# Input projection and gates as block products in a stage of their own, with outputs passed through HBM

## The chip, the cores and the metric

The kernel runs on one core of one Trainium2 chip. The metric is the device time of one execution in microseconds, the median of several runs. PE is TensorE's matmul unit, DVE VectorE, ACT ScalarE, POOL GpSimd and SP the engine that issues most transfers. HBM is the memory off the core, PSUM the memory that PE accumulates into.

## The reference

One layer of a decoder trunk for 512 prompt tokens (one sequence) and 64 sample tokens (8 sequences of 8), with the same weights, in fp32:

```python
xn = rmsnorm(h, lw['g_mix'])
z = xn @ lw['w_in']                                    # 1024 -> 512 + 1024 + 512
u_pool, u_rnn, q = ...
gates = jax.nn.sigmoid((xn @ lw['w_gate'] + lw['b_gate']))   # 1024 -> 3 x 1024
y_pool, new_pool = pool_mixer(u_pool, ...)
y_rnn, ... = rglru(u_rnn, ...)
y_attn = cross_attn(q, m_k, m_v)                       # m_k, m_v from 256 memory tokens
merged = (gates[:, :, 0] * (y_pool @ lw['w_br_pool'])
          + gates[:, :, 1] * (y_rnn @ lw['w_br_rnn'])
          + gates[:, :, 2] * (y_attn @ lw['w_br_attn']))
h = h + merged @ lw['w_out']
xn2 = rmsnorm(h, lw['g_ffn'])
gv = xn2 @ lw['w_up']
...
h = h + (jax.nn.gelu(g_conv) * val) @ lw['w_down']
```

The outputs are the two groups' normalised h, the memory keys and values, and the state rows that the convolutions, the pooling and the recurrence carry on.

## The kernel before

The 576 tokens lie along the free axis and features along the 128 partitions, so that x is 8 tiles of 128 x 576. All large matmuls take fp32 in two parts: `hi` is the value rounded to the type that PE takes in one pass (ACT copies it, L111), `lo` the value less `hi` (DVE, L112), and each product of 128 input features is three matmuls, wh·xh, wh·xl and wl·xh (`mm3`, L197). A column tile of 576 tokens is worked in two halves of 288 (or 256 and 320), so that one output tile of 128 features from all 1024 inputs is 8 x 3 x 2 = 48 matmuls.

The program has two stages. The mix stage holds the projections, the three branches, the gates and the merge, the second stage (`op_ffn`) the output projection, the second norm, the conv-FFN and the final norm. The order of the mix stage is written out in the string `MIX` (L1221), one letter for an operation and digits for its tile: `a` loads x and scales it by g_mix, `x` computes the reciprocal root mean square of each token (rstd), `r` and `p` are the projections of RG-LRU and pooling tiles, `g` a gate tile, `c R A B` the steps of the RG-LRU (convolution, its two gates, decay, scan), `w d o` those of pooling, `m K M k V` the memory keys and values, `Q S T P s t v z` attention, `b` a product of a branch with its weights, gated and merged. `h H` bring in x again and split the merged tiles. The builder's scheduler may move instructions of neighbouring operations past each other; each engine then runs its own list in order.

The projections multiply x scaled by g_mix but not by rstd, which comes in as each result leaves PSUM: `op_gate` multiplies by it on DVE (L492) and then takes the sigmoid on ACT (L493), `scaled_evac` does it for RG-LRU and pooling (L285, L288). So PE can begin on projections before any norm is known. Class `Weights` loads each weight tile of 512 KB on SP's queue (two raw buffers) and splits it on ACT and DVE (three buffers each for hi and lo). There are 16 tiles of `w_in` and 24 of `w_gate`. They and all tiles between stay in the core's own memory.

## Time and profile before

| what | value |
|---|---|
| median of 3 runs | 948.49 us (948.09 to 950.51) |
| the profiled execution, its own time | 947.94 us |
| span of the profiled execution | 946.0 us |
| PE busy in the span | 919.5 us (97%) |
| mean granted TensorE clock | 0.996 of 2.4 GHz |
| mix stage | 0 to 450.7 us |
| output projection to the end (`op_ffn`) | 450.7 to 946.0 us |

The span runs from the first to the last instruction of the core; the execution's time is 1.9 us longer. The listed length of a matmul overlaps that of its neighbours, so that what one costs is read where many stand in a row in the chain. PE is busy nearly throughout; the other engines have idle time in every stretch.

### The profile page before, as it was taken

The page shows a single profiled execution, that of the slowest core. Times are in us where ns is not written, and L with a number is a line of the kernel's source. Part 1 is how long each engine was busy: PE and PEld are TensorE (multiplying, and loading weights), DVE is VectorE, ACT ScalarE, POOL GpSimd, SP SyncE. Part 2 cuts the span into 40 slices and gives each one's busy share as a digit, 9 for nine tenths or more (in the row PEclk, how much of TensorE's full clock was granted, in tenths as well). Part 3 has the DMA queues.
Part 4 walks back from the last instruction along what each step waited for, and adds up shares of the span by engine and source line. Part 5 has one row for each costly group of instructions (what it writes and reads, how often), then busy time and mean ns, then how long its engine had stood idle before and what let it go on. Part 6 is the DMA issues. An engine that isn't in the chain of part 4 may idle for free.

```text
span 946.0 us, 17081 instructions
## 1 busy us (share of the span) xinstructions
PE 919.5 (97%) x6924; PEld 903.0 (95%) x6924; DVE 621.9 (66%) x974; ACT 472.2 (50%) x745; POOL 200.9 (21%) x302
## 2 busy tenths in 40 slices
PE   6999999999999999999999999999999999999995
PEld 6999999999999979899999999999999999999995
DVE  7979864656434656237466998676676676676644
ACT  6455948496222546325455465444444444444443
POOL 5224221127113110022222232111111111111131
PEclk9999999999999999999999999999999999999998
DMA  7422222344233353533637255454454454453202
GB/s 234 140 79 68 75 71 69 94 146 133 81 112 98 124 202 127 187 122 112 211 83 158 90 163 155 124 145 134 125 143 135 128 141 137 123 142 110 84 30 100
DMA packets 39662, 116.73 MB, mean 123 GB/s; under 512 B 4608, under 2 KB 8704, under 8 KB 39584
## 3 DMA queue, kind: packets, MB, share of 16 engines
q1 hardware_dynamic: 34496, 100.19, 31.3%
q0 software_dynamic: 4000, 14.28, 8.6%
q8 instruction: 54, 0.88, 0.4%
q10 hardware_dynamic: 1088, 1.18, 0.4%
q14 instruction: 24, 0.20, 0.1%
HBM read 111.58 MB, written 4.05 MB: 122 GB/s over the span
## 4 chain that ended last, share of the span: by engine, by line
PE 86%; DVE 6%; issue 2%; DMA 2%; ACT 2%; POOL 1%; SPq 0%; DVEq 0%; ACTq 0%; POOLq 0%
PE pb_ffn L901 25%; PE ps_gate L197 15%; PE pd_ffn L987 13%; PE ps_branch L197 10%; PE pb_ffn L806 5%; PE ps_rnn_mm L197 3%; PE ps_q L197 3%; PE pb_ffn L1134 3%; PE ps_pool_mm L197 2%; PE pq_rnn_gate L197 1%; PE pq_k_mm L197 1%; PE ps_v L557 1%; DMA cv_spv<-in_cv 1%; DMA wr_start<-in_w_gate 1%; DVE wl_ffn L112 1%
## 5 line engine op out<-in xcount | busy, mean ns | idle before, releaser
L901 PE MATMUL pb_ffn<-b_ffn,wh_ffn 128*128 128x288 f32 x768 | 155.3, 295 | 0.0
L901 PEld LDWEIGHTS pb_ffn<-b_ffn,wh_ffn 128*128 128x128 f32 x768 | 123.3, 188 | 0.1
L901 PE MATMUL pb_ffn<-b_ffn,sh_ffn 128*128 128x288 f32 x576 | 119.3, 299 | 2.4 <-DVE b_ffn L112 1.3
L901 PE MATMUL pb_ffn<-b_ffn,wl_ffn 128*128 128x288 f32 x384 | 112.9, 294 | 0.0
L901 PEld LDWEIGHTS pb_ffn<-b_ffn,sh_ffn 128*128 128x128 f32 x576 | 92.0, 188 | 4.4 <-DVE b_ffn L112 1.7
L901 PE MATMUL pb_ffn<-b_ffn,sl_ffn 128*128 128x288 f32 x288 | 84.7, 295 | 0.2 <-DVE sl_ffn L112 0.2
L901 PEld LDWEIGHTS pb_ffn<-b_ffn,wl_ffn 128*128 128x128 f32 x384 | 72.2, 188 | 0.0
L111 ACT ACTIVATE wh_ffn<-wr_ffn 128x1024 fp32r<-128x1024 f32 x44 | 46.7, 1061 | 39.0 <-PE pb_ffn L901 37.7
L111 ACT ACTIVATE sh_ffn<-R_ffn 128x512 fp32r<-128x512 f32 x72 | 45.0, 626 | 26.1 <-PE pb_ffn L901 19.4
L987 PE MATMUL pd_ffn<-xb_ffn,wh_ffn 128*128 128x288 f32 x320 | 55.7, 295 | 1.0 <-ACT xb_ffn L111 1.0
L987 PE MATMUL pd_ffn<-xa_ffn,wh_ffn 128*128 128x288 f32 x320 | 55.6, 295 | 0.0
L901 PEld LDWEIGHTS pb_ffn<-b_ffn,sl_ffn 128*128 128x128 f32 x288 | 54.1, 188 | 0.4 <-DVE sl_ffn L112 0.4
L112 DVE TENSOR_TENSOR wl_ffn<-wr_ffn,wh_ffn 128x1024 fp32r<-128x1024 f32 x44 | 54.1, 1230 | 0.2
L111 ACT ACTIVATE wh_branch<-wr_branch 128x1024 fp32r<-128x1024 f32 (+1 forms) x24 | 22.0, 917 | 62.7 <-PE ps_gate L197 27.4
L974 POOL TENSOR_TENSOR v_ffn<-v_ffn,ext_ffn 128x576 f32<-128x576 f32 x24 | 36.0, 1499 | 79.7 <-ACT ext_ffn L963 77.1
L112 DVE TENSOR_TENSOR sl_ffn<-R_ffn,sh_ffn 128x512 fp32r<-128x512 f32 x72 | 51.1, 711 | 0.6 <-ACT sh_ffn L111 0.6
L112 DVE TENSOR_TENSOR wl_ffn<-R_ffn,wh_ffn 128x1024 fp32r<-128x1024 f32 x22 | 26.9, 1224 | 36.4 <-ACT wh_ffn L111 36.4
L856 POOL DMA_DIRECT2D wr_ffn<-in_w_up x21 | 18.7, 892 | 142.5 <-DMA wr_ffn<-in_w_up 102.0
L111 ACT ACTIVATE wh_ffn<-R_ffn 128x1024 fp32r<-128x1024 f32 x22 | 23.3, 1060 | 50.8 <-PE pb_ffn L901 47.0
L987 PEld LDWEIGHTS pd_ffn<-xb_ffn,wh_ffn 128*128 128x128 f32 x320 | 46.8, 188 | 1.2 <-ACT xb_ffn L111 1.2
L987 PEld LDWEIGHTS pd_ffn<-xa_ffn,wh_ffn 128*128 128x128 f32 x320 | 46.9, 188 | 0.0
L959 DVE SCALAR_TENSOR_TENSOR gc_ffn<-ext_ffn,par,gc_ffn 128x592 f32<-128x592 f32 x48 | 41.4, 862 | 6.1 <-ACT gc_ffn L957 6.1
(510 smaller groups left out, 2434.8 us busy)
## 6 DMA issues: line engine op xcount, KB each, us to landing
R_ffn<-in_w_up SPq DMA_DIRECT2D x24, 512.0 KB, 3.8
wr_ffn<-in_w_down SPq DMA_DIRECT2D x24, 512.0 KB, 4.2
wr_ffn<-in_w_up SPq DMA_DIRECT2D x23, 512.0 KB, 3.7
wr_ffn<-in_w_up POOLq DMA_DIRECT2D x21, 512.0 KB, 6.3
R_ffn<-in_w_up SPq DMA_DIRECT2D x24, 256.0 KB, 4.0
wr_gate<-in_w_gate SPq DMA_DIRECT2D x10, 512.0 KB, 3.3
ck_sscore<-in_ck SPq DMA_DIRECT2D x8, 512.0 KB, 4.5
cv_spv<-in_cv SPq DMA_DIRECT2D x8, 512.0 KB, 5.0
```

Source lines behind the costliest of these rows:

```text
L111: nc.scalar.activation(hi, src, AF.Copy)
L112: nc.vector.tensor_tensor(lo, src, f(hi), ALU.subtract)
L197: nc.tensor.matmul(out[:, c, : hs.stop - hs.start], a[:, ks], b[:, hs], start=(first and k == 0 and i == 0), stop=(last and k == K - 1 and ...
L557: nc.tensor.matmul(vps[:, mt, :], a[:, ms], b[:, ws], start=(k == 0 and i == 0), stop=(k == 7 and i == 2))
L806: nc.tensor.matmul(p_[:, :TH], a[:, ks], x[:, b], start=(k == 0 and i == 0), stop=(k == 7 and i == 2))
L856: nc.gpsimd.dma_start(SR[j], w2(wu[j][:, 1:3]), accum_op=ALU.add)
L901: nc.tensor.matmul(p_[:, :TH], a[:, ks], b[:, k, :], start=(first and k == 0 and i == 0), stop=(k == 3 and i == 2), skip_group_check=not f ...
L959: nc.vector.scalar_tensor_tensor(gc[:, :592], ext[:, q_ : q_ + 592], pc(cw + q_), gc[:, :592], ALU.mult, ALU.add)
L974: nc.gpsimd.tensor_tensor(v, v, ext[:, :T], ALU.mult)
L987: nc.tensor.matmul(p_[:, c, :TH], a[:, ks], b[:, hs], start=(k == 0 and i == 0), stop=(k == NFB - 1 and i == 2),)
L1134: nc.tensor.matmul(p_[:, :n], a[:, ks], b[:, cs], start=(k == 0 and i == 0), stop=(k == NFB - 1 and i == 2),)
```

## The change

The 40 column tiles of `w_in` and `w_gate` become 20 pairs. Both stand as blocks: the weights of a pair as 2 x 2 (two halves of the inputs by two tiles), x as 2 x 2 (two halves of the inputs by two halves of 288 tokens). Each pair is computed by seven products of blocks (512 inputs x 128 outputs by 288 tokens) where the plain way has eight, from sums and differences of blocks: forms of x are made once (`N11 N21 N22 T1 T2 T3 T4`, negated or summed blocks, each split into hi and lo), those of the weights for each pair, and the seven results are added and subtracted, in PSUM where signs allow, otherwise as they leave it. A product is 4 x 3 = 12 matmuls of 288 columns.

- All of this stands in a new operation `op_xstage`, first in `MIX`. It begins with the memory keys and values (which came later before), loads x in two halves of tokens, and normalises each half before any product.
- Table `XP` gives the order of the 20 pairs (`g` gate, `r` RG-LRU, `p` pooling, `q` attention queries), table `XTRA` what is done beside which pair: the RG-LRU's and pooling's steps in pairs 4 to 18.
- For each pair, SP loads 512 KB and 256 KB of weights (`load_X`) and 512 KB for the sums (`load_S`), to which POOL's queue adds another 512 KB by an accumulating transfer. From pair 4 on, the low part of the upper weight blocks is no DVE subtraction: ACT writes hi, then -hi into lo, and a second accumulating transfer adds the weights (`prep_A`).
- Gates, queries, the RG-LRU's and pooling's results and the keys and values are stored to scratch in HBM (28 tiles of 128 x 576, 8 of 128 x 600, 4 of 128 x 576, and the keys and values). The 24 branch products and attention follow in a stage that loads them back; `op_gate` there is a load and a sigmoid.
- `op_ffn` keeps its work.

```diff
+NPX = 3
+XP = (
+    ("g", 0, 0), ("g", 0, 1), ("g", 0, 2), ("g", 0, 3), ("r", 0), ("p", 0), ("g", 1, 0), ("r", 1), ("g", 1, 1), ("p", 1),
+    ("r", 2), ("g", 1, 2), ("g", 1, 3), ("r", 3), ("q", 0), ("q", 1), ("g", 2, 0), ("g", 2, 1), ("g", 2, 2), ("g", 2, 3),
+)
+XTRA = {
+    (4, 0): "L", (5, 0): "c0", (5, 1): "c1", (6, 1): "R0 R1 A0 A1", (7, 0): "B0 B1", (7, 1): "w0 d0", (8, 0): "c2 o0",
+    (8, 1): "c3 w1 d1", (9, 1): "R2 R3 A2 A3 o1", (10, 0): "B2 B3", (10, 1): "w2 d2", (11, 0): "c4 o2", (11, 1): "c5",
+    (12, 0): "w3 d3", (12, 1): "R4 R5 A4 A5 o3", (13, 0): "B4 B5", (14, 0): "c6", (14, 1): "c7",
+    (15, 1): "R6 R7 A6 A7", (16, 0): "B6 B7", (17, 1): "y0 y1", (18, 1): "y2 y3",
+}
...
+        def load_X(j):
+            AR[j] = raw()
+            nc.sync.dma_start(AR[j], w2(wx[j][:, 2:4]))
+            A2[j] = fs.tile([P, 512], F32, tag="a22", name=nm("a22"), bufs=2)
+            nc.sync.dma_start(A2[j], wx[j][:, 0])
+
+        def load_S(j, tag="xa"):
+            SR[j] = xu(tag, [1152], F32)[:, :1024]
+            nc.sync.dma_start(SR[j], w2(wx[j][:, 0:2]))
+            nc.gpsimd.dma_start(SR[j], w2(wx[j][:, 1:3]), accum_op=ALU.add)
+
+        def prep_A(j):
+            WA[j] = hi, lo = ring()
+            if j <= NPX:
+                split_to(hi, lo, AR[j])
+            else:
+                nc.scalar.activation(hi, AR[j], AF.Copy)
+                nc.scalar.activation(lo, f(hi), AF.Copy, scale=-1.0)
+                nc.gpsimd.dma_start(lo, w2(wx[j][:, 2:4]), accum_op=ALU.add)
+
+        def prep_S2(j):
+            r = AR[j]
+            nc.vector.tensor_tensor(r[:, :512], r[:, :512], SR[j][:, :512], ALU.add)
+            W1[j, 6] = single()
+            split_to(*W1[j, 6], r[:, :512])
+
+        def prep_S(j):
+            WS[j] = ring()
+            split_to(*WS[j], SR[j])
+
+        def prep_22(j):
+            W1[j, 4] = single()
+            split_to(*W1[j, 4], A2[j])
+
+        def prep_S4(j):
+            r = AR[j]
+            nc.vector.tensor_tensor(r[:, 512:], r[:, 512:], r[:, :512], ALU.add)
+            W1[j, 3] = single()
+            split_to(*W1[j, 3], r[:, 512:])
+
+        def prod(p_, w, c0, x, first=True):
+            wh, wl = w
+            xh, xl = B[x]
+            for k in range(4):
+                ks = slice(c0 + k * P, c0 + (k + 1) * P)
+                for i, (a, b) in enumerate(((wh, xh), (wh, xl), (wl, xh))):
+                    nc.tensor.matmul(
+                        p_[:, :TH], a[:, ks], b[:, k, :],
+                        start=(first and k == 0 and i == 0), stop=(k == 3 and i == 2),
+                        skip_group_check=not first,
+                    )
...
+        def done(j):
+            kind, a = XP[j][0], XP[j][1:]
+            if kind in OFF:
+                return
+            for i in range(2):
+                n = 2 * a[-1] + i
+                name = f"q{n}" if kind == "q" else f"g{a[0]}{n}"
+                nc.sync.dma_start(spill(name, [P, T]), S.pop(("out", j, i)))
...
+        def P1(j):
+            C["b6", j] = bank()
+            prod(C["b6", j], WA[j], 0, "N11")
+            C["p1", j] = act_copy(C["b6", j])
...
+        def P4(j):
+            p_ = C.pop(("b6", j))
+            prod(p_, W1.pop((j, 4)), 0, "T4", first=False)
+            for o, sl in halves(j, 1, 0):
+                if j < NPX:
+                    nc.vector.tensor_tensor(o, sl(p_), sl(C["u2", j]), ALU.add)
+                else:
+                    nc.scalar.activation(o, sl(p_), AF.Copy)
+            del C["u2", j]
+            done(j)
...
+            else:
+                P1(j)
+                if more:
+                    prep_A(n)
+                P5(j)
+                if more:
+                    prep_S2(n)
+                P6(j)
+                P2(j)
+                if more:
+                    prep_S(n)
+                P7(j)
+                extras((j, 0))
+                P3(j)
+                if more:
+                    prep_22(n)
+                P4(j)
+                if more:
+                    prep_S4(n)
+                ld(n + 2, n + 3)
+            extras((j, 1))
...
     def op_gate(b, m):
-        p_ = wmm(("w_gate", 8 * b + m), S["xg"], H288)
-        g = (tg if b < 2 else te if m < 4 else ty)(T)
-        nc.vector.tensor_tensor(v2(g), p_[:, :, :TH], v2(S["rb"]), ALU.mult)
+        g = MD["gl"].tile([P, T], F32, tag="gl", name=nm("gl"))
+        nc.sync.dma_start(g, SP[f"g{b}{m}"])
         nc.scalar.activation(g, g, AF.Sigmoid, bias=pc(C_BG + 8 * b + m))
```

DVE's list at the start before: splits of the first weights (`wl_start`) and of x as it arrives (`xa_start`, `xb_start`); the norm (`e_rstd_x`) comes behind them.

```order
L112 TENSOR_TENSOR wl_start<-wr_start,wh_start 128x256 [waits DMAHW1_49,Activation_49]
L282 SCALAR_TENSOR_TENSOR xa_start<-e_start,par,xa_start 128x576 [waits DMAHW2_49,DMAHW0_49,Activation_49]
L112 TENSOR_TENSOR wl_start<-wr_start,wh_start 128x256 [waits DMAHW3_49,Activation_49]
L282 SCALAR_TENSOR_TENSOR xb_start<-e_start,par,xb_start 128x576 [waits DMAHW4_49,Activation_49]
L112 TENSOR_TENSOR wl_start<-wr_start,wh_start 128x256 [waits DMAHW5_49,Activation_49]
L282 SCALAR_TENSOR_TENSOR xa_start<-e_start,par,xa_start 128x576 [waits DMAHW6_49,Activation_49]
L112 TENSOR_TENSOR wl_start<-wr_start,wh_start 128x256 [waits DMAHW7_49,Activation_49]
L282 SCALAR_TENSOR_TENSOR xb_start<-e_start,par,xb_start 128x576 [waits DMAHW0_49,Activation_49]
L282 SCALAR_TENSOR_TENSOR xa_start<-e_start,par,xa_start 128x576 [waits DMAHW1_49,Activation_49]
```

DVE's list now, shortly before the first product of the main loop (`xb_`, `xa_xstage` with 1152 elements are blocks of x, `pd` the broadcast rstd, `sl` low parts of pair weights, `b_90` the low part of T2, `b_104` that of T3):

```order
L486 TENSOR_TENSOR xb_xstage<-xb_xstage,pd_xstage 128x1152 [waits PE_49]
L486 TENSOR_TENSOR xb_xstage<-xb_xstage,pd_xstage 128x1152 [waits DMAHW6_49]
L783 TENSOR_TENSOR xa_xstage<-xb_xstage,xa_xstage 128x1152 [waits DVE_49]
L116 TENSOR_TENSOR sl_xstage<-wr_xstage,sh_xstage 128x512 [waits Activation_49]
L784 TENSOR_TENSOR xb_xstage<-xb_xstage,xa_xstage 128x1152 [waits DVE_49]
L116 TENSOR_TENSOR sl_xstage<-wr_xstage,sh_xstage 128x512 [waits Activation_49]
L793 TENSOR_TENSOR xb_xstage<-xb_xstage 128x1152
L116 TENSOR_TENSOR b_90_xstage<-xb_xstage,b_89_xstage 128x1152 [waits Activation_49]
L116 TENSOR_TENSOR b_104_xstage<-xb_xstage,b_103_xstage 128x1152 [waits Activation_49]
```

These rows stand behind 53 others of the same list, the splits of the memory tokens and of the eight key and value weights, the squares of x and the first two forms. On PE, the first products of the pairs follow the memory matmuls, and product P6 of pair 0 (`b_89` and `b_90` are T2) takes what the list above ends with:

```order
L548 MATMUL pb_xstage<-b_60_xstage,wh_xstage 128x288 [waits PE_49,Activation_49]
L548 MATMUL pb_xstage<-b_61_xstage,wh_xstage 128x288
L548 MATMUL pb_xstage<-b_89_xstage,sh_xstage 128x288 [waits PE_49]
L548 MATMUL pb_xstage<-b_90_xstage,sh_xstage 128x288 [waits DVE_49]
L548 MATMUL pb_xstage<-b_89_xstage,sl_xstage 128x288
L548 MATMUL pb_xstage<-b_89_xstage,sh_xstage 128x288
L548 MATMUL pb_xstage<-b_60_xstage,wl_xstage 128x288 [waits DVE_49]
```

The second matmul of P6 waits for DVE's row of `b_90`.

ACT's list before around the two gates of RG-LRU tile 2 (`e_rnn_gate` from PSUM `pq_rnn_gate`; `hab` weights; `wh` high parts of weights; `e_rnn_a` the decay; ACT_TABLE_LOAD stands where the function's table changes):

```order
L409 ACT_TABLE_LOAD [waits PE_49]
L409 ACTIVATE e_rnn_gate_1035<-pq_rnn_gate_1036,par 128x300 [waits Pool_49]
L493 ACTIVATE g_gate_2_1032<-g_gate_2_1032,par 128x576 [waits DVE_49]
L409 ACTIVATE e_rnn_gate_1035<-pq_rnn_gate_1041,par 128x300 [waits PE_49]
L409 ACTIVATE e_rnn_gate_1046<-pq_rnn_gate_1047,par 128x300 [waits PE_49]
L111 ACTIVATE e_pool_d_1076<-pd_pool_d_1070 128x576
L409 ACTIVATE e_rnn_gate_1046<-pq_rnn_gate_1052,par 128x300 [waits PE_49]
L111 ACTIVATE hab_rnn_conv_1656<-rab_rnn_conv_1654 128x256 [waits DMAHW4_49]
L111 ACTIVATE wh_gate_3_1173<-wr_gate_3_1171 128x1024 [waits DMAHW7_49,PE_49,Activation_49]
L111 ACTIVATE e_rnn_conv_1152<-e_rnn_conv_1147 128x600 [waits DVE_49,Pool_49]
L111 ACTIVATE e_pool_d_1162<-pd_pool_d_1156 128x576
L418 ACT_TABLE_LOAD
```

ACT's list now, from the last evacuation of pair 6 (L677) on; `u_xstage` is the evacuation of a pair's product:

```order
L677 ACTIVATE xa_xstage<-pb_xstage 128x288 [waits PE_49]
L342 ACT_TABLE_LOAD
L342 ACTIVATE e_xstage<-pd_xstage,par 128x300 [waits PE_49] x2
L605 ACTIVATE u_xstage<-pb_xstage 128x288 [waits PE_49]
L342 ACTIVATE e_xstage<-pd_xstage,par 128x300 [waits PE_49] x2
L115 ACTIVATE hab_xstage<-rab_xstage 128x256 [waits DMAHW4_49]
L342 ACTIVATE e_xstage<-pd_xstage,par 128x300 [waits DMAHW3_49,PE_49]
L342 ACTIVATE e_xstage<-pd_xstage,par 128x300 [waits PE_49]
L342 ACTIVATE e_xstage<-pd_xstage,par 128x300 [waits DMAHW4_49,PE_49]
L351 ACT_TABLE_LOAD [waits Activation_49]
L351 ACTIVATE e_xstage<-e_xstage,nsp_88 128x600 [waits Pool_49]
L342 ACT_TABLE_LOAD
```

The gates of two tiles now follow each other with few other rows between them, and the evacuations of the next pair's products (L605) stand in the same list. Up to the last evacuation of pair 7 there are 31 instructions in this interval: 4 evacuations of 288 columns, 8 sigmoids of 300, 5 table loads, 2 exponentials, 2 tangents, 2 squares and 2 square roots of 600, and copies of 1024, 576, three of 512 and one of 256.

PE in a steady pair before, one gate:

```order
L197 MATMUL ps_gate_0_522<-xa_start,wh_pool_mm_376 128x288 x4
L197 MATMUL ps_gate_0_522<-xa_start,wl_pool_mm_377 128x288 x2
L197 MATMUL ps_gate_0_522<-xb_start,wh_pool_mm_376 128x288 x4
L197 MATMUL ps_gate_0_522<-xb_start,wl_pool_mm_377 128x288 x2
L197 MATMUL ps_gate_0_522<-xa_start,wh_pool_mm_376 128x288 x2
```

and now, from the end of one pair to the start of the next (`b_115`, `b_116` T4; `b_60`, `b_61` N11; `wl` the low part that the accumulating transfer fills):

```order
L548 MATMUL pb_xstage<-b_116_xstage,sh_xstage 128x288
L548 MATMUL pb_xstage<-b_115_xstage,sl_xstage 128x288
L548 MATMUL pb_xstage<-b_60_xstage,wh_xstage 128x288
L548 MATMUL pb_xstage<-b_61_xstage,wh_xstage 128x288
L548 MATMUL pb_xstage<-b_60_xstage,wl_xstage 128x288 [waits DMASW7_49]
L548 MATMUL pb_xstage<-b_60_xstage,wh_xstage 128x288
L548 MATMUL pb_xstage<-b_61_xstage,wh_xstage 128x288
```

The third matmul of a pair's first product waits for a transfer on a POOL queue (DMASW); the weights' low part before came from DVE.

## Rows read from the trace of the kernel before

**Rows 1.** The page: span, and busy time of each engine

```profile
span 946.0 us, 17081 instructions
...
PE 919.5 (97%) x6924; PEld 903.0 (95%) x6924; DVE 621.9 (66%) x974; ACT 472.2 (50%) x745; POOL 200.9 (21%) x302
```

**Rows 2.** Stretches: PE, PEld, DVE, ACT, POOL busy (x); clock; DMA share; GB/s

```profile
0.00:24.00 24.00, 15.72 (x85) 14.31 (x85) 17.21 (x25) 16.27 (x26) 12.05 (x36) 1.00 0.70 231
...
100.00:150.00 50.00, 50.00 (x373) 49.67 (x373) 35.47 (x46) 35.09 (x52) 11.08 (x20) 1.00 0.23 70
...
400.00:451.00 51.00, 49.76 (x372) 49.32 (x371) 28.63 (x42) 20.59 (x35) 11.40 (x6) 1.00 0.39 127
```

**Rows 3.** The chain that ended last, 0 to 60 us: start, us, what

```profile
5.45 6.63 DMA wr_start<-in_w_gate
...
34.79 6.40 PE ps_rnn_mm L197 x48
```

**Rows 4.** The same chain from 300 to 455 us

```profile
302.93 5.67 PE pq_k_mm L197 x48
...
323.26 11.14 PE ps_v L557 x48
...
450.69 4.39 PE pb_ffn L806 x31
```

**Rows 5.** The longest wait of PE up to 451 us: total, times, longest

```profile
PE ps_rnn_mm L197 <- ACT xa_start L281: 5.9, 1, 5.9
```

**Rows 6.** ACT by shape: busy us, mean ns of one | idle before it

```profile
L111 ACT ACTIVATE sh_ffn<-R_ffn 128x512 fp32r<-128x512 f32 x72 | 45.0, 626 | 26.1 <-PE pb_ffn L901 19.4 <-DVE R_ffn L873 6.3
...
L111 ACT ACTIVATE wh_gate<-wr_gate 128x1024 fp32r<-128x1024 f32 x16 | 16.9, 1057 | 19.3 <-PE ps_branch L197 8.4 <-PE ps_rnn_mm L197 5.3 <-issue 4.3
L409 ACT ACTIVATE e_rnn_gate<-pq_rnn_gate,par 128x300 f32<-128x300 f32 x32 | 15.2, 507 | 3.4 <-PE pq_rnn_gate L197 3.1
...
L913 ACT ACTIVATE u_ffn<-pb_ffn 128x288 f32<-128x288 f32 x24 | 9.8, 410 | 16.0 <-PE pb_ffn L901 16.0
...
L409 ACT ACT_TABLE_LOAD x5 | 6.4, 1283 | 0.1
L418 ACT ACTIVATE e_rnn_a<-e_rnn_gate,nsp 128x600 f32<-128x600 f32 x8 | 6.4, 797 | 0.1
...
L420 ACT ACTIVATE e_rnn_gate<-e_rnn_a 128x600 f32<-128x600 f32 x8 | 5.6, 701 | 0.2
```

**Rows 7.** DVE by shape, columns as in the group before

```profile
L112 DVE TENSOR_TENSOR wl_ffn<-wr_ffn,wh_ffn 128x1024 fp32r<-128x1024 f32 x44 | 54.1, 1230 | 0.2
L112 DVE TENSOR_TENSOR sl_ffn<-R_ffn,sh_ffn 128x512 fp32r<-128x512 f32 x72 | 51.1, 711 | 0.6 <-ACT sh_ffn L111 0.6
...
L112 DVE TENSOR_TENSOR b_ffn<-hr_ffn,b_ffn 128x1152 fp32r<-128x1152 f32 x4 | 5.3, 1350 | 0.0
...
L282 DVE SCALAR_TENSOR_TENSOR e_mem<-e_mem,par 128x256 fp32r<-128x256 f32 x8 | 4.6, 593 | 1.8 <-ACT e_mem L281 1.8
```

**Rows 8.** ACT in order of time: start us, us, what

```profile
204.57 1.04 ACT L111 ACTIVATE wh_gate<-wr_gate 128x1024 fp32r<-128x1024 f32 x1
205.63 1.28 ACT L409 ACT_TABLE_LOAD   x1
206.93 0.51 ACT L409 ACTIVATE e_rnn_gate<-pq_rnn_gate,par 128x300 f32<-128x300 f32 x1
207.33 0.79 ACT L419 ACTIVATE e_rnn_a<-e_rnn_gate,sp 128x600 f32<-128x600 f32 x1
```

**Rows 9.** The page: DMA queues (packets, MB, share); one issue (KB, us to landing)

```profile
q1 hardware_dynamic: 34496, 100.19, 31.3%
q0 software_dynamic: 4000, 14.28, 8.6%
...
wr_ffn<-in_w_up POOLq DMA_DIRECT2D x21, 512.0 KB, 6.3
```

**Rows 10.** The last 21 us, columns as in the second group

```profile
925.00:946.00 21.00, 11.16 (x85) 10.53 (x84) 9.42 (x23) 6.74 (x16) 3.68 (x5) 0.82 0.33 112
```

More of the change, by code (lines that the diff above doesn't have):

```diff
@@ new lines, in tile_hybrid_decoder_step, with load_yp, op_open_mix, pool @@
+    y_pool = [None] * 4
+    y_rnn = [None] * 8
+    def load_yp(g):
+        r = te(T)
+        nc.sync.dma_start(r, SP[f"yp{g}"])
+        t = xu("xb", [2, T])
+        y_pool[g] = t[:, 0], t[:, 1]
+        split_to(*y_pool[g], r)
+    def op_open_mix():
+        mix = S["mix"] = ExitStack()
+        def pool(name, bufs, **kw):
+            return mix.enter_context(tc.tile_pool(name=name, bufs=bufs, reuse_waits="tile", **kw))
+        ua, gl, ue = pool("ua", 1), pool("gl", 5), pool("ue2", NUE2)
+        psp = pool("psp", 3, space=PSUM)
+        MD["u"] = ua
+        MD["gl"] = gl
+        MD["e"] = lambda w=UW, dt=F32: ue.tile([P, UW], dt, tag="e", name=nm("e"))[:, :w]
+        MD["q"] = lambda: psp.tile([P, 512], F32, tag="pq", name=nm("pq"), bufs=2)
+        MD["s"] = lambda: psp.tile([P, 2, 512], F32, tag="ps", name=nm("ps"))
+        phase.close()
+        S["at"] = phase.enter_context(tc.tile_pool(name="at", bufs=2, **right))
+        for g in range(2):
+            qmask[g] = S["at"].tile([P, 544], F32, tag=f"qm{g}", name=nm("qm"), bufs=1)
+            nc.gpsimd.memset(qmask[g], 0.0)
@@ new lines, in op_k, with op_v, op_q @@
+    def op_k(hp):
+        r = te(512)
+        nc.sync.dma_start(r, SP[f"k{hp}"])
+        kT[hp] = split(r, 512)
+    def op_v(mt):
+        r = te(512)
+        nc.sync.dma_start(r, SP[f"v{mt}"])
+        vT[mt] = split(r, 512)
+    qs = [None] * 4
+    qmask = [None] * 2
+    def op_q(h):
+        qt = te(T)
+        nc.sync.dma_start(qt, SP[f"q{h}"])
+        for g in range(2):
+            nc.gpsimd.tensor_copy(sview(qmask[g], h * P, 40, 4)[:, :, 0:8], sview(qt, NP_ + 32 * g, 8, 4))
+        qs[h] = split(qt[:, :NP_], NP_)
@@ L745, in op_ffn @@
     def op_ffn():
-        mix.close()
+        S["mix"].close()
         ff = ExitStack()
```

625 lines of the change are left out of this document (403 added, 222 removed), and 8 rows, old and new, of the table OPS.

## The prediction

> **What bounds the kernel now.** I read the page's busy times first, then stretches, then the chain that ended last. PE is busy 919.5 of 946.0 us [rows 1]. In a full stretch of the mix stage it has no idle time at all: 50.00 of 50 us, with DVE at 35.5, ACT at 35.1 and the DMA engines at a share of 0.23 [rows 2]. So PE is the bound, its clock is the full 2.4 GHz there (granted 1.00), and the other engines have about 30% to spare in that stretch. What one matmul costs is read in the chain, where 48 stand in a row: 6.40 us for one column tile of 576 tokens, 133.3 ns for each [rows 3]. The mix stage ends at 450.69 [rows 4]; what follows is not changed. In it PE waits long only once, 5.9 us for the first x [rows 5]; the first 24 us hold 85 matmuls, which at 133.3 ns are 11.3 us of work, so that the start costs 12.7 us of idle time [rows 2].
>
> **What PE gains.** Forty column tiles of 48 matmuls are 1920. Twenty pairs of seven products of twelve are 1680, all of 288 columns. 240 matmuls fewer at 133.3 ns are -32.0 us. The norm's broadcasts for two halves in place of one add less than 1 us. Branches, attention, memory and RG-LRU matmuls stay. I take **-31**. This is the whole gain; everything else decides how much of it is kept.
>
> **The start.** Before, a product could begin once one tile of x and one of weights were split. Now x is squared, normalised, added and subtracted before any product, and pair 0 comes to P6 only when DVE has written the low part of T2. Ahead of that in DVE's list, and with it, stand 12 operations of 1152 elements, 9 of 1024, 10 of 512, 8 scaled splits and 4 subtractions of 256, and some 17 tiny ones. At 1350, 1230, about 700, 593 and about 400 ns [rows 7] and about 0.1 for a tiny one that is 16.2 + 11.1 + 7.0 + 4.7 + 1.6 + 1.7 = 42.3 us. Instructions that follow each other overlap a little: ACT's copy that begins at 204.57 with 1.04 is followed at 205.63, but the sigmoid of 206.93 with 0.51 at 207.33, 0.11 before its end [rows 8]; 0.09 for each of 60 takes the sum to 37. DVE begins when the first transfers land, near 5.5 us, the time at which the chain leaves the issues for a transfer [rows 3]. So P6 starts no earlier than 42, with no wait at all in DVE's list. PE's work ahead of it is 96 matmuls of 256 columns and 48 of 512 for keys and values, 5.67 and 11.14 us for each 48 [rows 4], so 22.5, and some four products of 12, 6 to 8 us: 30. That leaves 12 us of idle time as the floor. DVE's list also waits for ACT's splits, for the norm's round trip over PE, ACT and DVE, and for about 10 MB that have to be in by then; P7 then needs T3 and the first sums of weights, which stand behind. I take 22 us of idle time, bounds 13 and 32. Against 12.7 before: **+9**, 0 to +19.
>
> **ACT in the RG-LRU pairs.** ACT had 15 of 50 us free [rows 2]. Now it evacuates four of the seven products and makes high parts for summed weights, and from pair 4 on writes lo = -hi too. The RG-LRU's gates stand in four bursts, each with two tiles. From the last evacuation of pair 6 to that of pair 7: 4 evacuations at 410 ns, 8 sigmoids at 507, 5 table loads at 1283, 2 exponentials and 2 tangents at about 790, 4 squares and roots at 701, copies of 1024 (1057), 576 (about 690), three of 512 (626) and one of 256 (about 410) [rows 6]: 22.1 us, 19.3 with an overlap of 0.09 for each of the 31. PE needs 84 x 0.133 + 24 gate matmuls at about 0.138 (a little over the 133.3 of 288 columns) = 14.5 us for the same interval. PE runs ahead only as far as the four PSUM banks of a pair allow; P5 of the next pair wants the bank that this pair's P4 leaves, one product, 1.6 us. So a burst holds PE 4.8 - 1.6 = 3.2 us, four of them 13, if ACT has no slack left from before; with listed lengths 6.0 each, 24. Against it: ACT's work comes in the order of its list, and the gates of a pair may run before PE is at the evacuations that they would delay. I take **+8**, bounds 0 and +24.
>
> Of ACT's five table loads in a burst, the row shows 1.28 us, and the sigmoid behind it begins 1.30 after its start [rows 8]. The Trainium skill (ScalarE: Activation LUTs, What ACT_TABLE_LOAD costs) gives 1283 ns and a drain of about 1380 more, 2.66 us for each switch. By that figure a burst would be 6.9 us longer, four 28, and the sum would end near +18 instead of -10. The row, in which nothing stands between load and next activation, speaks against it; it stays a rival.
>
> **DMA.** A full stretch used 0.23 of the DMA engines; a gate pair now loads 1.31 MB, stores 0.59 MB and adds 1.05 MB in two accumulating transfers. The hardware queue took 31.3% of 946 us for 100.19 MB, 2.96 us for 1 MB; the software queue, most of whose bytes are accumulating transfers, 8.6% for 14.28 MB, 5.70 for 1 MB [rows 9]. A gate pair then takes 5.6 + 6.0 = 11.6 us of all 16 engines beside 11.2 us of PE. Over the whole stage it is about 47 MB (139 us) and 36 accumulations of 0.52 MB (108 us), 247 us beside about 263 of PE: nearly full, but within it, and the pairs with RG-LRU steps leave 3 us each. A transfer is needed two pairs after its issue: -hi (two ACT copies, 2.1 us), issue about 0.9 and landing 6.3 [rows 9] are 9.3 us, with 14 at hand. Pairs 0 to 3 and 16 to 19 are gates in a row and may fall behind: 8 x 0.4 = 3. **+2**, bounds 0 and +15, the upper one if queues delay each other by 0.8 us in each pair.
>
> **Evacuation, stores and the branch stage.** DVE loses 24 gate multiplications and gets three or four evacuations of 288 for each pair; from pair 6 to 16 its list, at the same prices, is about 119 us beside 128 of PE. That is hidden unless ACT is late. The issues of stores are hidden on SP, which does nothing else. At the border some 15 tiles of 0.3 MB come back and are split before the first branch product, 4.5 MB or 13 us of the engines; those of the first products are issued while the last pair is at work. Attention, split among gates before, is split among branch products now; its 48-matmul pieces still lie between its steps. **+2**, bounds -3 and +6.
>
> **Sum:** -31 + 9 + 8 + 2 + 2 = -10. On the span of 946.0 that is 936; the execution is 1.9 longer than its span, 938. Its 947.94 stand 0.5 under the median of the runs, so that the gain is about 10 us of 948.49. A difference under 0.3%, 2.8 us, I count as no change.
>
> **Rivals.**
> - *All is hidden.* Start 13, no stall: -31 + 0 to 4, so 917 to 921. For it: 30% free on every other engine; against it, DVE's floor of 42 us and four bursts beyond PE's pace. Chance 0.13.
> - *ACT and the start take it all (slower).* The place is P5 and P1 of the pair behind each of the four bursts: PE waits for ACT, and because ACT then is late with hi and -hi, the next accumulating transfer starts late too. At the upper prices 24 + 12 to 19 for the start, less 31: +5 to +14, 953 to 962. It decides once start and bursts together cost over 31. For it: three engines each near 100% in one stretch; against it, work between bursts is shorter than PE's 11.2 us. Chance 0.22.
> - *The DMA engines become the bound.* 11.6 against 11.2 us per gate pair, and any loss of rate pushes the P1 wait (its wl). At 0.9 of the rate the 247 us become 274, 11 over PE's 263, and at +15 in place of 2 the sum is 951: 947 to 951. For it: a share of 0.23 becomes 0.94; against it: the average still fits. Chance 0.12.
> - *The clock falls in the sparse start.* The last 21 us, PE busy 11.2, were granted 0.82 [rows 10]; the first 24 us, PE busy 15.7, 1.00 [rows 2]. A start with 30 of 52 us busy is between them. At 0.82 for 30 us, +5 on the sum: 943. The rule in the Trainium skill (TensorE: Matmul & The Clock Gate) that idle time drops the clock bears on this; the last stretch agrees, the first doesn't show it. Chance 0.05.
> - *Table loads with a wait behind them.* If each held ACT twice its row, 6.4 us per burst and 26 in all: about 964. The row speaks against it. Chance 0.03.
>
> **Numbers.** The forecast has 0.45, its own range is 927 to 948. Faster: 0.41 of it, 0.13 hidden, 0.01 of others: 0.55. Same: 0.04, and 0.09 of the rivals, most of it the DMA engines': 0.13. The rest, 0.32, slower. The range leaves out the lower half of "hidden" and the top of the slower cases: 921 to 962.
>
> **What would show it.** -31: the projections' matmuls are 1680, with 6.4 us for 48. Start: P6 of pair 0 (matmuls on T2) begins between 47 and 60 us, and what releases it is DVE's L116. Bursts: waits of PE on ACT's evacuations (L605, L677) or high parts (L115) behind pairs 6, 9, 12 and 15, 2 us each; if they are none, my ACT sum is wrong. DMA: share 0.9 to 1.0 in the gate pairs and few waits of PE on wl; many such waits and PE's pace over 12 us in pairs 16 to 19 show the rival. The output projection should begin near 441.

## The result and the profile after

The changed kernel takes 1039.07 us (median of 4 runs, 1036.31 to 1043.06) beside 948.29 us before (947.49 to 950.51): 1.096 times as long, 95% interval 1.091 to 1.100. The forecast was 938 with a range of 921 to 962. The profiled execution took 1036.31 with a span of 1034.4 us, 88 us over the span of before and 98 over the 936 of the forecast.

The page of the changed kernel: busy times, two of its lines in 40 slices (tenths; PEclk is the granted clock), the two queues (packets, MB, share), and the weight transfers (count, KB, us from issue to landing).

```profile
PE 929.7 (90%) x6724; PEld 904.3 (87%) x6724; DVE 667.9 (65%) x1097; ACT 568.5 (55%) x928; POOL 203.7 (20%) x322
...
PEclk9889999988899998989989999999999999999998
DMA  7939866857676578651654444654444454545112
...
q1 hardware_dynamic: 50864, 130.28, 37.3%
q0 software_dynamic: 9504, 34.20, 18.0%
...
wr_xstage<-in_w_x SPq DMA_DIRECT2D x20, 512.0 KB, 7.8
xa_xstage<-in_w_x SPq DMA_DIRECT2D x19, 512.0 KB, 4.7
xa_xstage<-in_w_x POOLq DMA_DIRECT2D x19, 512.0 KB, 9.2
wl_xstage<-in_w_x POOLq DMA_DIRECT2D x16, 512.0 KB, 7.6
```

PE's share of the span has gone from 97% [rows 1] to 90%; its clock is under 0.9 in 9 of the 40 slices. The accumulating queue has more than doubled in bytes. A raw weight block of 512 KB (`wr`) takes 7.8 us to land (3.7 where the page of before has the same size on SP's queue in the FFN); accumulating transfers take 7.6 and 9.2 where they took 6.3 [rows 9]. The first block of a pair's sums (`xa`), of the same size and on the same queue of SP, lands in 4.7, so that the 7.8 do not hold for every load of the stage.

The same kernel in four stretches: start, products, branch stage, output projection to the end (columns as in the second group of rows of before).

```profile
0.00:70.00 70.00, 47.74 (x264) 42.64 (x265) 41.50 (x63) 42.07 (x69) 14.07 (x47) 0.92 0.72 228
70.00:372.00 302.00, 258.12 (x1748) 250.49 (x1748) 198.40 (x332) 195.90 (x310) 67.25 (x102) 0.93 0.70 183
372.00:532.00 160.00, 136.98 (x1099) 128.07 (x1097) 83.45 (x168) 93.74 (x178) 29.59 (x26) 0.94 0.60 204
532.00:1034.00 502.00, 486.89 (x3618) 483.06 (x3618) 344.49 (x536) 236.78 (x372) 92.79 (x147) 0.99 0.44 125
```

The last product ends at 372.2, the output projection begins at 531.9, and from there on it takes 502.5 us where it took 495.3. Set against the working of the forecast:

| stretch | forecast | measured | off by |
|---|---|---|---|
| start to P6 of pair 0 | 31 of work + 22 idle = 53 | 69.7 | +17 |
| P6 to the last product | 233 of work + 8 (ACT) + 2 (DMA) = 243 | 302.5 | +59 |
| branch stage | 122 of work + 21 idle as before + 2 = 145 | 159.7 | +15 |
| output projection to the end | 495.3 | 502.5 | +7 |

Work is counted in matmuls at the prices of the rows of before. The 21 us called idle are what is left of before's 450.7 after 12.7 of start and 417 of work; they are no measured waits: from 24 us to that border the trace of before has PE idle for under 5 us, and the rest stands in small matmuls and in 23 of the output projection. The four differences make up the 98 us. The table shows where they lie, not why.

One border is not the same on both sides. In the kernel before the first matmul of the output projection begins at 446.1 us, 4.6 before the 450.7 that the table uses; in the changed kernel 531.9 is the first matmul. Counted alike, the last stretch takes 499.9 before and 502.5 after, and is off by under 3 us; the branch stage is off by 19.

### The profile page after: what moved, and what is told of

Read it like the earlier page. It is cut to its first block, busy times and chain, and to the rows that moved or that the text cites. A ratio compares the mean times of both kernels' runs of the same rounds, so it can differ in the third digit from the quotient of the medians.

```text
span 1034.4 us, 17349 instructions
## 1 busy us (share of the span) xinstructions
PE 929.7 (90%) x6724; PEld 904.3 (87%) x6724; DVE 667.9 (65%) x1097; ACT 568.5 (55%) x928; POOL 203.7 (20%) x322
## 4 chain that ended last, share of the span: by engine, by line
PE 63%; DMA 12%; ACT 9%; DVE 7%; issue 5%; POOL 2%; SPq 1%; DVEq 0%; ACTq 0%; POOLq 0%
PE pb_ffn L1269 23%; PE pd_ffn L1355 12%; PE pb_xstage L548 11%; DMA wr_xstage<-in_w_x 6%; PE pb_ffn L1174 5%; PE ps_branch L194 4%; PE pd_xstage L194 3%; PE pb_ffn L1502 2%; DMA wl_xstage<-in_w_x 2%; DMA gl_gate<-sp_g 1%; POOL g_branch L929 1%; DVE sl_xstage L116 1%; ACT L351 1%; DMA e_xstage<-in_pool_w 1%; DMA cv_spv<-in_cv 1%
## 5 line engine op out<-in xcount | busy, mean ns | idle before, releaser
L548 PE MATMUL pb_xstage<-b_xstage,wh_xstage 128*128 128x288 f32 x640 | 139.2, 309 | 13.4 <-ACT wh_xstage L115 9.3
L548 PE MATMUL pb_xstage<-b_xstage,sh_xstage 128*128 128x288 f32 x480 | 104.9, 311 | 20.6 <-ACT u_xstage L605 12.3
L548 PEld LDWEIGHTS pb_xstage<-b_xstage,wh_xstage 128*128 128x128 f32 x640 | 110.1, 200 | 15.2 <-ACT wh_xstage L115 9.7
L548 PE MATMUL pb_xstage<-b_xstage,wl_xstage 128*128 128x288 f32 x320 | 98.1, 307 | 10.8 <-DMA wl_xstage<-in_w_x 10.8
L548 PEld LDWEIGHTS pb_xstage<-b_xstage,sh_xstage 128*128 128x128 f32 x480 | 82.1, 200 | 23.2 <-ACT u_xstage L605 13.6
L548 PEld LDWEIGHTS pb_xstage<-b_xstage,wl_xstage 128*128 128x128 f32 x320 | 63.6, 199 | 12.3 <-DMA wl_xstage<-in_w_x 12.0
L548 PE MATMUL pb_xstage<-b_xstage,sl_xstage 128*128 128x288 f32 x240 | 73.4, 306 | 0.0
L116 DVE TENSOR_TENSOR wl_ffn<-wr_ffn,wh_ffn 128x1024 fp32r<-128x1024 f32 x44 | 54.1, 1229 | 0.2
L116 DVE TENSOR_TENSOR sl_ffn<-R_ffn,sh_ffn 128x512 fp32r<-128x512 f32 x72 | 52.2, 727 | 0.6 <-ACT sh_ffn L115 0.6
```

Of the source, the lines that this page charges most:

```text
L116: nc.vector.tensor_tensor(lo, src, f(hi), ALU.subtract)
L548: nc.tensor.matmul(p_[:, :TH], a[:, ks], b[:, k, :], start=(first and k == 0 and i == 0), stop=(k == 3 and i == 2), skip_group_check=not f ...
```

## The experiments

Each ran once, with a profile, beside a run of the kernel before on the same chip (947.7 to 950.6 us). The changed kernel's own runs lie 7 us apart, so that differences under 5 us are not told apart. The times of stages are read from each profile.

Three theories stood at the beginning. *Late weights*: transfers of a pair land too late, ACT's list stands still in front of them, and the evacuations behind them in that list hold PE. *Stores*: the stores of gates and queries hold SP's list and buffers. *ACT's load*: the bursts of the prediction. PE's waits up to the first matmuls of the output projection alone don't decide between them (us in total, times, longest):

```profile
PE pb_xstage L548 <- ACT u_xstage L605: 16.2, 7, 3.8
PE pb_xstage L548 <- DMA wl_xstage<-in_w_x: 10.8, 5, 4.6
PE pb_xstage L548 <- ACT wh_xstage L115: 9.3, 2, 7.7
...
PE pb_ffn L1174 <- ACT xb_msplit L115: 5.9, 1, 5.9
PE pq_spv L1068 <- DMA cv_spv<-in_cv: 5.7, 2, 3.9
```

The largest is a wait for ACT's evacuation, but the chain that ended last names transfers (start, us, what):

```profile
36.59 7.10 DMA wr_xstage<-in_w_v
...
46.13 7.57 DMA wr_xstage<-in_w_x
...
69.05 13.40 PE pb_xstage L548 x85
84.83 9.41 DMA wr_xstage<-in_w_x
...
118.16 10.24 DMA wr_xstage<-in_w_x
133.43 8.76 DMA wr_xstage<-in_w_x
...
182.77 8.67 DMA wl_xstage<-in_w_x
...
244.34 8.57 DMA e_xstage<-in_pool_w
...
395.79 5.00 DMA wr_branch<-in_br_rnn
...
416.45 3.64 DMA ck_sscore<-in_ck
...
430.56 5.26 DMA gl_gate<-sp_g
...
448.00 4.62 DMA cv_spv<-in_cv
```

What hides behind ACT's name is seen in ACT's list in order of time:

```profile
121.01 0.39 ACT L605 ACTIVATE u_xstage<-pb_xstage 128x288 f32<-128x288 f32 x1
122.07 1.06 ACT L115 ACTIVATE wh_xstage<-xa_xstage 128x1024 fp32r<-128x1024 f32 x1 [0.67 <-PE pb_xstage L548]
128.47 1.06 ACT L518 ACTIVATE wh_xstage<-wr_xstage 128x1024 fp32r<-128x1024 f32 x1 [5.34 <-DMA wr_xstage<-in_w_x]
129.57 1.06 ACT L519 ACTIVATE wl_xstage<-wh_xstage 128x1024 fp32r<-128x1024 f32 x1
...
131.05 0.87 ACT L326 ACTIVATE e_xstage<-e_xstage,par 128x600 f32<-128x600 f32 x1
...
132.64 0.69 ACT L605 ACTIVATE u_xstage<-pb_xstage 128x288 f32<-128x288 f32 x2
```

At 123.1 ACT is done with the sums of the next pair and stands for 5.34 us in front of the weight block that SP issued at 118.16 and that lands at 128.40 (in the chain). The evacuations `u_xstage`, of results that PE's next products wait to see gone, come six places behind it in the list, at 132.64. The load of 244.34 shows the same on a small scale: 64 KB of pooling weights, loaded for each tile now, land after 8.57 us, and PE stands for 6.7 us (246.6 to 253.3) in front of the product that takes them.

The accumulating transfer of a pair is held in another way. POOL's list around one, then ACT's:

```profile
180.20 2.00 POOL L366 COPY so_h<-e_xstage 128x9 f32<-128x9 f32 x2 [1.31 <-DVE e_xstage L365]
182.15 0.67 POOL L323 COPY so_rnn<-e_xstage 128x27 f32<-128x27 f32 x1
182.77 0.89 POOL L520 DMA_DIRECT2D wl_xstage<-in_w_x  x1
```

```profile
175.26 1.30 ACT L360 ACTIVATE e_xstage<-e_xstage 128x600 f32<-128x600 f32 x2
...
180.07 1.06 ACT L518 ACTIVATE wh_xstage<-wr_xstage 128x1024 fp32r<-128x1024 f32 x1
...
181.31 1.07 ACT L519 ACTIVATE wl_xstage<-wh_xstage 128x1024 fp32r<-128x1024 f32 x1
```

The accumulating transfer at 182.77 stands behind POOL's copies of RG-LRU states, but these cost it 0.4 us at most: ACT had written -hi (L519) only at 182.4. The raw block had landed at 168.7; ACT began its copy (L518) 11.4 us later, behind the RG-LRU burst (L360 is one of its rows). The transfer lands 8.67 us after its issue and PE waits for it (in the chain).

**e1_no_store**

```diff
-                nc.sync.dma_start(spill(name, [P, T]), S.pop(("out", j, i)))
+                S.pop(("out", j, i))
...
-        nc.sync.dma_start(g, SP[f"g{b}{m}"])
+        nc.sync.dma_start(g, A["xT"][:, m, :])
...
```

> The 28 stores of gates and queries are left out and the branch stage loads rows of x in their place (wrong values, same loads), beside a changed kernel of about 1039 us. If the stores are the cause (they stand in SP's list ahead of the weight loads, and hold the buffers that the weight sums need): 40 us or more faster. If late weights behind the accumulating transfers are the cause: 10 to 20 faster, since 8.3 MB, about 24 us of the DMA engines, are gone. If ACT's own load is the cause: within 5.

1028.65 us, 10 faster than the changed kernel's median, products done at 362.9 (372.2). That is the lower end of what the removed transfer time alone was to give (10 to 20); stores as the main cause are out.

**e2_split_A**

```diff
-            if j <= NPX:
+            if j < 99:
                 split_to(hi, lo, AR[j])
```

> All pairs get the low part of the upper weight blocks from DVE (hi on ACT, subtraction on DVE), none from an accumulating transfer; nothing else changes. Late weights: 30 to 60 us faster, because the chain from load to first product loses a transfer of about 8 us and the DMA engines lose 48 us of work. ACT's load: 10 to 15 faster (16 copies of 1.06 fewer). Stores: at most 10 faster.

1012.89 us, 26 faster, products done at 349.9. That lies between what late weights (30 to 60) and ACT's load (10 to 15) foretold. ACT's waits for weight blocks from 70 to 338 us fell from 30.9 to 16.7 us, and the blocks land in 6.2 us (7.8).

**e3_no_S_add**

```diff
-            nc.gpsimd.dma_start(SR[j], w2(wx[j][:, 1:3]), accum_op=ALU.add)
```

> The accumulating transfer that forms the weight sums is left out (the sums are then only the first block, wrong values); all else stays. Late weights: 30 to 50 us faster, 60 us of the DMA engines' work is gone and the loads of the next weights land sooner. ACT's load or stores: at most 10 faster.

1023.27 us, 16 faster, under the 30 to 50 of late weights, although 60 us of the DMA engines' time were gone. If the capacity of the DMA engines were the bound of the whole stage, this edit should have been the best of the three. In its fullest part, 115 to 143 us, their share is 0.89; what capacity costs there no run tells apart.

**e4_no_tables**

```diff
-nc.scalar.activation(t[:, hs], p_[:, :300], AF.Sigmoid, bias=pc(bc + n))
+nc.scalar.activation(t[:, hs], p_[:, :300], AF.Identity, bias=pc(bc + n))
...
-nc.scalar.activation(th[:, :RW], th[:, :RW], AF.Sqrt)
+nc.scalar.activation(th[:, :RW], th[:, :RW], AF.Square)
```

> In the RG-LRU steps sigmoid, exponential, tangent and root are replaced by identity and square of the same shapes (wrong values), so that the pairs hold no table load. ACT's load: 40 us or more faster, 20 table loads are 26 us and what they hold behind them. Late weights: 5 to 15 faster. Stores: no change.

1015.46 us, 24 faster, products done at 353.0; PE's wait for evacuations fell from 16.2 to 6.3 us. Between the theories again: the 20 table loads are about 26 us, and about as much came back. The kernel before has table loads too, 27 from 70 to 372 us where the changed one has 21, so that the gain tells what ACT's list is worth here, and not what the change added to it. Each of the four edits is worth something, and none is the cause alone.

**e5_all_four**: the four edits in one kernel.

> All four edits before at once: no stores of gates and queries (rows of x loaded in their place), the split of all pairs on DVE, no accumulating transfer at all, no table loads in the RG-LRU steps (wrong values). The single gains against 1039 were 10, 26, 16 and 24, in sum 76. If they are different places that each hold PE: about 965. If they are one place that several causes reach (each edit alone only uncovers the next): the pairs run at PE's pace once all are gone and the gain is more than the sum, 950 or less. If something else holds the pairs that none of them touches: 985 or more.

981.63 us, 57 faster, less than the sum of 76 and more than any one: partly the same waits. The stretches of its products and its branch stage:

```profile
67.00:312.00 245.00, 239.92 (x1748) 235.77 (x1747) 208.14 (x348) 155.38 (x274) 45.63 (x65) 0.99 0.39 124
312.00:478.00 166.00, 138.68 (x1098) 129.95 (x1097) 81.30 (x168) 93.20 (x178) 29.65 (x27) 0.93 0.57 192
```

The products now end at 312.2, 60 us earlier, and 245.6 us after P6 of pair 0 for 233 us of work: with these four gone, PE keeps nearly its pace at a clock of 0.99 and a DMA share of 0.39. So these four things together hold 57 of the 59 us of the table's second line. The branch stage has not changed (166.0), and the kernel is still 33 us slower than before.

**e6_one_kv_weight**

```diff
+        def kvw():
+            if "kvw" not in S:
+                S["kvw"] = W.get(("w_k", 0))
+            return S["kvw"]
...
-                w = W.get(("w_k", 2 * hp + e))
+                w = kvw()
...
```

> The memory keys and values use one weight tile for all eight (wrong keys and values, all matmuls stay): 3.7 MB fewer loads and seven splits fewer on ACT and DVE before the first product. If the start waits for transfers and splits of weights: 12 to 20 us faster. If it waits for the norm and the forms of x on DVE: at most 5 faster.

1031.02 us, 8 faster; P6 of pair 0 begins at 59.6 in place of 69.7. The time lies between the two theories. So 10 us of the start are key and value weights that land late (7.10 us at 36.59 in the chain) and their splits. What the remaining 60 us hold beside DVE's instructions (busy for 36 us up to P6 in this run) was not tried apart.

**e7_gates_square**

```diff
-        nc.scalar.activation(g, g, AF.Sigmoid, bias=pc(C_BG + 8 * b + m))
+        nc.scalar.activation(g, g, AF.Square, bias=pc(C_BG + 8 * b + m))
```

> In the branch stage the gates' sigmoid is a square of the same shape (wrong values), so that sigmoid and exponential no longer change tables there (16 loads fewer). If the table changes are what holds the branch stage: 15 to 25 us faster. If it is the loads of gates and the merge on POOL: at most 5 faster.

1033.55 us, 5.5 faster, hardly more than the kernel's own spread; the branch stage 152.7 in place of 159.7. Table changes are some 7 us of it, and not the 15 to 25 of the first theory.

**e8_raw3**

```diff
-NUY, NUG, NUE, NUE2 = 16, 13, 12, 13
+NUY, NUG, NUE, NUE2 = 16, 13, 11, 13
...
-            AR[j] = raw()
+            AR[j] = raw() if j % 3 < 2 else fs.tile([P, 1024], F32, tag="raw3", name=nm("wr"), bufs=1)
```

> Three buffers in place of two for the raw upper weight blocks of the pairs (one work tile fewer, 11 for 12, to make room), so that their load can be issued a pair earlier; values as in the changed kernel. If the weights are late because the two buffers let the load go out late: 15 to 30 us faster. If they are late because the DMA engines or the queues in front are full: at most 5 faster.

1027.36 us, 12 faster, between the two theories. ACT's long waits for the weight block are gone from its list of waits, but those of PE for the accumulating transfer grew from 10.8 to 13.8 us: the lateness moved one link on.

**e9_gates_not_loaded**

```diff
-        nc.sync.dma_start(g, SP[f"g{b}{m}"])
-        nc.scalar.activation(g, g, AF.Sigmoid, bias=pc(C_BG + 8 * b + m))
+        nc.scalar.activation(g, ident[:, :1].to_broadcast([P, T]), AF.Sigmoid, bias=pc(C_BG + 8 * b + m))
```

> The branch stage takes the sigmoid of a tile that is in the core's memory already (wrong values); the 24 loads of gates are left out, the stores stay. If the loads coming back hold the branch stage (38 us of idle time on PE there): 15 us or more faster than 1039. If what holds it is attention's own chain and the merges, which had gate matmuls beside them before and have none now: at most 6 faster.

1039.08 us, no change; the branch stage 160.4. The gate load that stands in the chain at 430.56 holds nothing that would not wait anyway.

**e10_all_six**: edits of e5, e6 and e9 together.

> All that was left out or replaced so far, together: no stores of gates and queries, no gate loads, no accumulating transfers, no table loads in the RG-LRU steps, one weight tile for keys and values (wrong values). The four together ran 982, the single weight tile is worth 8. If the rest is the start's norm and forms and attention without gate matmuls beside it: 960 to 975, still slower than before. If the remainder was transfers too: 948 or less.

967.94 us, 71 faster, still 20 slower than before: the start's forms of x and attention remain (P6 at 57.4, products done at 303.6, branch stage 160.7).

**e11_split_raw3_dve**: edits of e2, e8 and e12 together; nothing is left out.

> The changed kernel with right values and three of its choices altered: all low parts by DVE, three raw weight buffers, merges of branches on DVE. If the first two shorten different waits: 39 us faster, about 1000 with nothing from the merges. If they shorten the same wait: 26 faster, about 1012.

1002.87 us, 36 faster, about the sum of e2 and e8: they shorten different waits. It is the fastest run that computes the whole layer, and it is 55 us slower than the kernel before.

**e12_merge_dve**

```diff
-OPT = {"hp": 100, "ahead": 2, "madd": "P"}
+OPT = {"hp": 100, "ahead": 2, "madd": "D"}
```

> The merges of the branches (16 additions of 128 x 576) run on DVE in place of POOL, where one takes 1.75 us; nothing else changes. If the chain of merges and gate buffers at the end of the branch stage holds PE: 8 to 12 us faster. If not: within 4.

1037.33 us, no change; the branch stage 158.5. The merges hold nothing.

So the branch stage took 153 to 166 us whatever was taken from it, for 122 us of work. Of the 38 us between (159.7 less 122), its row in the four stretches shows 23 as PE's idle time (136.98 busy of 160); the rest lies in matmuls that took longer, at a mean granted clock of 0.94. The next four runs ask what these 38 us belong to.

**f1_fill**

```diff
...
+        if b:
+            pf = MD["s"]()
+            for i in range(24):
+                nc.tensor.matmul(pf[:, i % 2, :288], fill[:, :128], fill, start=i < 2, stop=i > 21)
```

> The changed kernel with 16 x 24 extra matmuls of 288 columns in the branch stage, on a constant tile, behind the gate tiles of the second and third branch; nobody reads them. They are 51 us of work on PE. Lost cover: most of them fall into waits, at most 25 us slower than 1039. A chain that bounds the stage by itself on PE's list: about 51 slower.

1078.77 us, 40 slower: inconclusive. The order of its instructions explains why: most of the added matmuls stand as whole blocks of 24 beside branch products, where PE did not wait, and only some between the steps of attention. 11 of 51 us fitted in by the whole time; the branch stage alone grew from 159 to 193 us, at a mean granted clock of 0.99 where it had 0.94.

**f2_before_no_g2**, in the kernel before:

```diff
-        p_ = wmm(("w_gate", 8 * b + m), S["xg"], H288)
+        p_ = None if b in (2,) else wmm(("w_gate", 8 * b + m), S["xg"], H288)
...
```

> The kernel before without the matmuls and weights of the eight gates of the third branch, which stand beside attention (the gates are made from rstd, wrong values): 51 us of work on PE are gone. Lost cover: only 20 to 35 us faster than 948, since attention's waits come to light. If attention has no waits that these matmuls fill: 50 faster.

930.25 us, 20 faster for 51 us of PE's work left out: 31 us of waits and of lower clock came to light. In the kernel before, 240 of the 384 matmuls left out stand among attention's steps (347 to 400 us), the others among the last branch products. The stretch around attention in the kernel before, then in this one:

```profile
350.00:400.00 50.00, 48.04 (x466) 42.98 (x465) 22.31 (x62) 22.82 (x59) 0.00 (x0) 1.00 0.47 156
```

```profile
350.00:400.00 50.00, 35.70 (x304) 27.68 (x305) 22.65 (x64) 25.12 (x64) 1.74 (x1) 0.80 0.47 158
```

DVE, ACT and the DMA share are alike; PE's busy time falls from 48.0 to 35.7 us and the granted clock from 1.00 to 0.80. Not all of the loss lies at attention: from the first matmul of the output projection to the end this kernel takes 510.7 us (from 417.4), where the kernel before takes 499.9 and the changed one 502.5.

**f3_before_no_gates**: the same edit with `b in (0, 1, 2)`.

> The kernel before without the matmuls and weights of all 24 gates: 154 us of PE's work gone, and 24 weight tiles on SP, ACT and DVE. Lost cover: 100 to 130 us faster, the rest comes to light as waits of the RG-LRU steps and attention. No cover in them: 150 faster.

863.62 us, 87 faster for 154 us of PE's work: less than both theories had said. More waits came to light than expected, the longest 9.6 us for a result of pooling. So the cover of the gates was not attention's alone.

**f4_no_attention**

```diff
     def op_score(hp, i):
+        return
...
+                for u in t:
+                    nc.vector.tensor_copy(u, ident[:, :1].to_broadcast([P, T]))
```

> The changed kernel without attention (scores, softmax, transposes and value products of both groups; constants in place of their results, wrong values); branches, gates, loads of queries, keys and values stay. About 19 us of PE's work are left out. If the idle time of the branch stage belongs to attention's steps: 40 us or more faster than 1039, the stage at most 120 us. If it belongs to the branches' loads, splits and merges: 15 to 25 faster, the stage about 140.

989.26 us, 50 faster; the branch stage, from the last product at 378.4 to the output projection at 480.1, takes 101.7 us:

```profile
378.00:480.00 102.00, 101.50 (x774) 101.08 (x773) 56.35 (x86) 52.05 (x84) 24.45 (x22) 1.00 0.67 227
```

PE is busy 101.5 of 102 us at full clock: 768 branch matmuls at 133.3 ns are 102.4. About 19 us of attention's matmuls are left out (by the prices of before), and 58 us went from the stage. Some 5 us of these moved on: the wait for the split merged tiles (5.9 in the waits above) now stands behind the border, 5.2 us. By the whole time, 50 less 19, 31 us of loss went with attention. With its steps the edit also left out its 16 loads of cached keys and values (512 KB each), so that steps and loads are not told apart; PE's waits for the values' loads are 5.7 us in the changed kernel.

## Why the prediction was wrong

**The gain** was sized right. 240 matmuls are gone, and where PE flows, 91 of the listed matmuls take 12.0 us, 132 ns each (fence below). In e5 the products run 13 us over their work, in f4 the branches at theirs.

**DMA and ACT, the step that failed most.** Put at +2 and +8, they hold the 59 us of the products. "A transfer is needed two pairs after its issue: ... 9.3 us, with 14 at hand" counted the accumulating transfer with the landing time of before, and not the weight load in front of it. That load goes out only when a pair has given back one of two raw buffers, in a burst with stores and two accumulating transfers, and takes 7.8 us in the median and up to 10.2; then hi and -hi 2.1, issue 0.9, accumulation 7.6. That is 18.4 to 20.8 us beside two pairs' 22.4, without a wait in any list. The shares of the engines (0.70 in the products) said nothing of it. The remark in the Trainium skill (DMA: Bandwidth & Descriptors, Issuing engines are not separate DMA queues), that transfers issued by ScalarE, SyncE and GpSimd run on the same 16 DMA engines and interleave, agrees with the landing times of both queues, which grew together.

The price of ACT's burst was about right, as far as e4 tells: 24 us for taking the table loads out lies at the upper bound that was given (0 to +24). What was left out is that ACT's list also stands still, 25.2 us in front of weight blocks (its waits for L518), and that evacuations stand behind.

DMA and ACT were two terms of a sum, each with the other one on time; in the trace each delay of the one is handed to the other. From issue of the raw block to landing of the accumulation it took 14.2 to 23.5 us in twelve of the pairs 4 to 19, and 31.9 to 33.7 in pairs 9, 12, 15 and 18. In these four ACT began hi 8.8 to 11.4 us after the block had landed, because its RG-LRU bursts stood in front, and PE's waits for an accumulating transfer end with just these four (4.6, 1.0, 2.7 and 2.2 of the 10.8 us). So the raw block is late for ACT by its landing, and the accumulating transfer is late for PE by ACT. The second rival had this mechanism ("because ACT then is late with hi and -hi, the next accumulating transfer starts late too") at 953 to 962. Its place was right, its price and chance were far too low.

The rival of the DMA engines as the bound was to show itself by many waits for the low part and a pace over 12 us in pairs 16 to 19. The pace came (58 us for the four), but at a share of 0.57 in these 58 us, so that full engines are not what held these pairs.

**The start.** P6 began at 69.7 and not at 47 to 60. DVE began at 5.4, as forecast, though by luck: the 5.45 of [rows 3] is the start of a transfer of 6.63 us and not its landing. It was busy for 41 us up to P6, where 37 had been counted, so that this floor was sized nearly right; what failed are the 22 us of idle time, 39 in the run. Up to 54 the chain is key and value weights and the first raw block landing 7.1 and 7.6 us after issue. e6 puts 10 of the 17 us on those; the other 7 were not tried apart. Nor was it DVE's L116 that released PE in front of P6, as the forecast had it:

```profile
69.05 0.85 PE L548 MATMUL pb_xstage<-b_xstage,wh_xstage 128*128 128x288 f32 x2 [7.68 <-ACT wh_xstage L115]
69.70 0.68 PE L548 MATMUL pb_xstage<-b_xstage,sh_xstage 128*128 128x288 f32 x2
```

The first two matmuls wait for ACT's copy of a weight block (67.96 to 69.00), which stands in ACT's list behind the high parts of the forms of x; P6 comes behind them.

**The branch stage.** The step "Attention, split among gates before, is split among branch products now; its 48-matmul pieces still lie between its steps" is the second that failed: the forecast let these waits stay as they were and put the whole stage at +2 (up to +6); counted from the same border it is off by 19. Before, gates lay beside attention as well, now only branch products do. f2 shows from the side of before that eight gates alone covered 31 us, 11 of them at the output projection and behind it (510.7 beside 499.9); f4 shows that 31 us of the changed kernel's loss go with attention and its loads. Reloads of gates, tables and merges, the first suspects, are worth 0, some 7 and nothing.

**The clock** was a rival with 0.05 and 5 us in the start. It fell in many of the places where PE waited. After 4.5 us without work (95.1 to 99.6):

```profile
95.00:100.00 5.00, 0.46 (x3) 0.40 (x3) 4.64 (x8) 2.94 (x5) 0.00 (x0) 0.98 0.75 191
99.60:102.50 2.90, 2.87 (x12) 2.90 (x13) 2.58 (x4) 0.26 (x1) 0.00 (x0) 0.53 0.75 295
103.00:115.00 12.00, 12.00 (x91) 12.00 (x91) 8.98 (x29) 6.71 (x11) 0.86 (x1) 0.99 0.66 171
```

At a granted 0.53 (1.2 GHz nearly throughout), 12 matmuls take 2.9 us, 240 ns each, and at 0.99 132. A mean of 0.93 over the products' 302 us is worth up to 21 us of the 59 (0.07 of 302). It follows from the waits: in e5, without most of them, it is 0.99.

**Table loads** were weighed against the 2.66 us for a switch in the Trainium skill (ScalarE: Activation LUTs, What ACT_TABLE_LOAD costs). The trace after agrees with the row of before, and not with that figure:

```profile
165.43 1.28 ACT L342 ACT_TABLE_LOAD   x1
166.72 0.51 ACT L342 ACTIVATE e_xstage<-pd_xstage,par 128x300 f32<-128x300 f32 x1
167.13 0.79 ACT L352 ACTIVATE e_xstage<-e_xstage,sp 128x600 f32<-128x600 f32 x1
```

The load takes 1.28 us, and the next activation begins 1.29 after the load's start; no drain is seen.

**The range**, 921 to 962, took ACT and the start to their upper bounds together, and the others not. Even all upper bounds together (-31 + 19 + 24 + 15 + 6 = +33) end at 981, so that it was not the choice within bounds that failed: ACT and DMA together cost 59 where their bounds add to 39, and the branch stage 19 where its bound was 6.

## What to carry to other kernels

Removing work from the engine that bounds a kernel gains what it costs only if the other engines and the transfers have time in that very stretch; add up the latencies of a whole chain from buffer release to use, at the landing times under the new load, and not the shares of each engine. Ask of work that moves what waits it covered where it stood: gate matmuls that nobody waited for had hidden much of attention. And where several engines come near full together, a list that waits in order hands its delay on, so that terms worked out one by one are too small.
